# One stage change of a two-layer decoder trunk written out in a fixed order on PE, ACT and DVE

## The chip, the cores and the metric

The kernel runs on one core of one Trainium2 chip. The metric is the device time of one execution in microseconds (us). PE is TensorE (matmul), DVE VectorE, ACT ScalarE, POOL GpSimd, SP the engine that issues the DMAs.

## The reference, cut to what matters

```python
x = sandwich(x, mixer, ...)        # layer 1: mixer = dilated_attention
x = sandwich(x, ffn_second, ...)   # layer 1: swiglu, D_FF = 2816

def sandwich(x, fn, pre_g, post_g, shift, scale, gate, res_w):
    hn = rmsnorm(x, pre_g) * (1 + scale) + shift
    y = rmsnorm(fn(hn), post_g)
    return x + res_w * gate * y

def dilated_attention(h, w_in, w_o, rel_bias):
    ...                                     # three dilations, mixed by their lse
    return o.reshape(B, S, 1024) @ w_o      # 512 tokens, 1024 features

def swiglu(h, w_gate, w_up, w_down):
    return (silu(h @ w_gate) * (h @ w_up)) @ w_down
```

Six such sub-layers run one behind the other (FFN, MLA, FFN, FFN, dilated attention, FFN). All is float32; the kernel splits each operand of a large product into two float32r parts, hi and lo, and sums three products.

## The kernel before

Tokens are the 512 columns, in four tiles of 128 (`TT`); features are 8 tiles of 128 (`KT`). A weight of 128x1024 is loaded by SP (`load`, L124, five `raw` buffers), copied to `whi` by ACT (L134) and subtracted to `wlo` by DVE in two halves (L136); six `whi` and six `wlo` buffers are there. `mm3` (L149 to L151) makes the three products. PSUM has four banks `mm` and four `aux`.

The place of the change is the **transition** behind the dilated stage. The stage's output is `o`, eight pieces (hi and lo each), times `w_o`: for each token tile i and half d of the features, eight times three products of 512 columns. `Mixer.part` makes the first four of the eight (`early`) while attention still runs and DVE copies them to SBUF tiles `y` (L467); `Mixer.tail` makes the rest, and DVE adds (L465). The eighth piece of `o` comes last, from a chain of DMAs and `put_o` (ACT L711, DVE L712). Then, tile by tile: squares on ACT (L316), `y` times the gate (DVE L477), a power on POOL for the root (L324), the residual stream `x` (DVE L505), squares of `x`, and `y` = `x` scaled by its own root (ACT L339 and DVE L340). When two tiles are scaled, PE transposes them (`turn`, L529, 16 transposes), and `modulate` makes `h`, hi and lo, out of each of the eight transposed pieces: DVE L311, ACT L312, DVE L313, or for two of the pieces ACT twice and POOL (L307 to L309).

The next FFN starts with **head units**: unit u is gate and up of 128 hidden features, 48 products over a half of the tokens (256 columns), then silu on ACT (L585), the product (DVE L587), and hi and lo of it (ACT L588, POOL or DVE L590). Three units (`HEAD`) are made in halves, the first half of tokens as soon as tiles 0 and 1 are turned; the others over all 512 columns. Unit 0's weights come in slices (`Sliced`: ACT L67, DVE L71).

Up to the end of `Dil.rest` the order on PE, ACT and DVE is that of the program (`manual_schedule`). In `transition` a scheduler orders these three engines by what it expects to be ready; only SP keeps the program's order.

```python
def transition(self, sub, nxt):        # L479
    ...
    for i in range(TT):
        sub.tail(i)
        self.tile_done(nxt, i)
        if nxt and i % 2:
            self.after(TURN, lambda i=i: self.turn(nxt, i - 1))
    ...
    for lo in (0, HT):
        for u in range(nxt.heads):
            nxt.head(u, lo, lo + HT)
```

Of the kernel before, what the change touches and what calls it, by code (L numbers as in the profile page):

```python
# [14 lines left out]
P = 128  # L15
# [12 lines left out]
UB = 4  # L28
SB = 4
HOT = 400  # L30
HEAD = 3
SPARE = (2, 3)
TURN = 26
START = 4
# [42 lines left out]
class Trunk:  # L77
# [401 lines left out]
    def transition(self, sub, nxt):  # L479
# [15 lines left out]
                    nxt.head(u, lo, lo + HT)  # L495
        self.count(4 * TURN if not nxt or not nxt.late else 0)

    def tile_done(self, nxt, i):

        nc = self.nc  # L500
        r = self.scale_of(self.ss)
        for d in range(2):
            c = slice(d * SEQ, (d + 1) * SEQ)
            x = self.x[i][:, c]
            nc.vector.scalar_tensor_tensor(x, self.y[i][d], r, x, ALU.mult, ALU.add)  # L505
            if not nxt:
                nc.sync.dma_start(self.a["out"][i][:, c], x)
        if nxt:
            self.normal(i, self.y[i])
            if nxt.parks:  # L510
                self.park(i)
# [26 lines left out]
class Ffn:  # L538
# [34 lines left out]
    def gate_up_out(self, ft, lo, hi, banks):  # L573
        t, nc = self.t, self.t.nc
        q = self.group(ft)
        j = ft - GROUPS[q][0]
        if q not in self.g:
            self.g[q] = [[], []]
        if j == len(self.g[q][0]):
            for x in self.g[q]:  # L580
                x.append(t.s(F32R))
        ghi, glo = [x[j][:, lo:hi] for x in self.g[q]]
        n = hi - lo
        s = t.t("silu")[:, :n]
        nc.scalar.activation(s, banks[0], AF.Silu)  # L585
        v = t.t("gg")[:, :n]
        nc.vector.tensor_tensor(v, s, banks[1], ALU.mult)  # L587
        nc.scalar.activation(ghi, v, AF.Copy)  # L588
        eng = nc.gpsimd if n < SEQ and ft < HEAD else nc.vector
        eng.tensor_tensor(glo, v, f(ghi), ALU.subtract)  # L590

    def head(self, ft, lo, hi):
# [38 lines left out]
    def rest(self):  # L631
        t = self.t
        last = len(GROUPS) - 1
        for q, (at, n) in enumerate(GROUPS):
            if q == last - 1:
                t.gates(self)
            for ft in range(max(at, START if t.first is self else HEAD), at + n):
                self.head(ft, 0, SEQ)
                t.pump(3 if t.first is self else 2)
            for i in range(TT if q < last else 0):  # L640
                self.down(q, i)
# [22 lines left out]
class Mixer:  # L664
# [11 lines left out]
    def products(self, b, i, d, js):  # L676
        t = self.t
        for j in js:
            self.out_weights(j)
            t.mm3(  # L680
                b,
                [x[j][:, i * P : (i + 1) * P] for x in self.o],
                [x[:, d * SEQ : (d + 1) * SEQ] for x in self.wo[j]],
                j in (0, self.early),
                j in (self.early - 1, KT - 1),
            )

    def part(self, n):

        i, d = divmod(n, 2)  # L690
        b = self.t.bank()
        self.products(b, i, d, range(self.early))
        self.t.y_part(i, d, b, True, self.busy)

    def tail(self, i):
# [21 lines left out]
class Mla(Mixer):  # L717
# [3 lines left out]
    busy = False  # L721
    early = 3
    waiting = 1
    w_o = "mla_o"

    def head(self, u, lo, hi):
# [242 lines left out]
class Dil(Mixer):  # L969
# [2 lines left out]
    late = False  # L972
    busy = True
    early = 4
    waiting = 1
    w_o = "dil_o"
    BLOCKS = (
        (0, ((0, 384, 128, 0), (1, 256, 256, 0))),
# [457 lines left out]
    def rest(self):  # L1436
        t = self.t
        t.gates(self)
        self.of = []
        self.bias = {}  # L1440
        self.coming, self.raws = self.loads(), []
        self.fetched = self.loaded = self.at = 0
        with t.tc.manual_schedule(engines={PE, ACT, DVE}):
            self.ahead(SLOTS - 2)
            self.biases(0)
            for p in range(7):
                values = [(p, g, j) for g in range(3) for j in range(4) if p in self.BLOCKS_V]
                for n, at in enumerate([(p + 1, u) for u in self.ORDER] + values):
                    self.fetch(self.at + SLOTS + 1 + max(n - 6, 0) % 4)
                    self.slot(p, n)  # L1450
                    self.ahead(self.at + min(SLOTS - 1 + max(n - 6, 0) % 4, SLOTS))
                    self.beside(p, n)
                    if n < 6:
                        self.tile(*at, 0, SEQ)
                    else:
                        self.value_tile(*at)
                    self.behind(p, n)
                    if n < 6 or n % 4 == 1:
                        self.at += 1 if n < 6 else 4
            self.fetch(self.at + SLOTS + 3)  # L1460
            self.slot(7, 0)
            self.ahead(self.at + SLOTS - 1)
            for x in self.of[:4]:
                self.put_o(x)
            self.tile(7, 2, 0, SEQ)
            self.slot(7, 1)
            self.ahead(self.at + SLOTS + 1)
            self.norm_out(self.pairs[6])
            t.new_y()
            self.part(0)  # L1470
            self.later()
            for x in self.of[4:]:
                self.put_o(x)
            self.part(1)
            last = self.pairs[7]
            self.tops(last)
            self.exps(7, (2,))
            self.tops_back(last)
            for i in range(2):
                t.unpark(i)  # L1480
            self.finish(6)
            self.put_o(self.of[-1])
            for n in range(2, 6):
                self.part(n)
            self.exps(7, (3,))
            self.norm_far(last)
            self.exps(7, (0, 1))
            self.norm(last)
            self.turn(7, 2)
            self.part(6)  # L1490
            self.turn(7, 3)
            self.part(7)
            self.turn(7, 0)
            self.weigh(7, 2, 2, 1)
            self.turn(7, 1)
            for n in (3, 0):
                self.weigh(7, n, 2, 1)
            self.norm_out(last)
            self.weigh(7, 1, 2, 1)
            for i in range(2, TT):  # L1500
                t.unpark(i)
            self.finish(7)
            self.put_o(self.of[-1])


def build(tc, a, plan):
    with ExitStack() as ctx:
        t = Trunk(ctx, tc, a)
        subs = [{"ffn": Ffn, "mla": Mla, "dil": Dil}[kind](t, l, i) for kind, l, i in plan]
        first = subs[0]  # L1510
        t.todo = [
            (s.l, 3 * s.i + n, k)
            for s in subs
            for n in ((2,) if s is first else range(3))
            for k in range(KT)
        ]
        with tc.manual_schedule(engines={SP}):
            t.start(first)
        for s, nxt in zip(subs, subs[1:] + [None]):
            with ExitStack() as order:  # L1520
                if s.parks:
                    order.enter_context(tc.manual_schedule(engines={SP}))
                s.rest()
                t.transition(s, nxt)


def bucket(dist):
# [98 lines left out]
```

## Time and profile before

| | |
|---|---|
| median of 3 runs | 2248.38 us (2247.44 to 2249.25) |
| the profiled execution | 2244.7 us, span 2242.9 us |
| PE busy | 2214.4 us, 99% of the span |
| DVE, ACT, POOL busy | 1180.5, 847.5, 109.1 us |
| the transition | about 1842 to 1892 us from the span's start |

The span runs from the first to the last instruction; 1.8 us lie around it. Times in the rows below count from the span's start. Idle time of an engine other than PE costs nothing by itself.

### The profile page before, as it was taken

Reading aid. Unit: us, or ns where it says so; the run is one execution under the profiler, and the core shown is the slowest. Engines: PE = TensorE matmul, PEld = TensorE weight load, DVE = VectorE, ACT = ScalarE, POOL = GpSimd, SP = SyncE. Lnnn points to the kernel's source line nnn. Section 1 sums busy time; section 2 is a strip of 40 time slices with the busy share of each in tenths; the row PEclk is TensorE's granted clock in tenths of the full one; section 3 lists DMA queues with packets and bytes.
Section 4 is the critical chain, followed back from the end, with each engine's and each line's share of the span. In section 5 each row is a group of like instructions: output and inputs, shape, how many; then the busy total and the mean of one; then the engine's idle time right before and its main releaser. Section 6 shows DMA issues by size and latency. Waiting matters only on the chain.

```text
span 2242.9 us, 30146 instructions
## 1 busy us (share of the span) xinstructions
PE 2214.4 (99%) x11354; PEld 1865.8 (83%) x11354; DVE 1180.5 (53%) x2691; ACT 847.5 (38%) x1730; POOL 109.1 (5%) x143
## 2 busy tenths in 40 slices
PE   7999999999999999999999999999999998999998
PEld 5888888977898888898888889888899888888887
DVE  7666565677655356474454464234523467333344
ACT  4432234587633132353222353425342446322232
POOL 0000001210110000020000010000000002000000
PEclk9999999999999999999999999999999999999999
DMA  8575762311255365434654523323342334333231
GB/s 309 158 248 181 200 220 74 109 54 57 69 167 185 106 188 179 131 117 135 181 172 129 160 98 103 112 90 97 85 131 68 104 86 138 92 116 102 76 113 38
DMA packets 124057, 290.34 MB, mean 129 GB/s; under 512 B 44786, under 2 KB 49157, under 8 KB 123910
## 3 DMA queue, kind: packets, MB, share of 16 engines
q1 hardware_dynamic: 123910, 288.41, 41.6%
q8 instruction: 89, 1.46, 0.3%
q14 instruction: 58, 0.48, 0.1%
HBM read 281.76 MB, written 4.49 MB: 128 GB/s over the span
## 4 chain that ended last, share of the span: by engine, by line
PE 92%; ACT 2%; DVE 2%; issue 2%; DMA 1%; POOL 1%; SPq 0%; POOLq 0%; DVEq 0%; ACTq 0%
PE mm L149 28%; PE mm L150 28%; PE mm L151 28%; PE mm L882 1%; PE aux L1298 1%; PE mm L1131 1%; PE aux L1265 1%; PE aux L931 1%; POOL mv L324 1%; PE aux L910 1%; PE aux L529 1%; PE aux L1131 0%; DVE x L505 0%; ACT whi L134 0%; PE aux L150 0%
## 5 line engine op out<-in xcount | busy, mean ns | idle before, releaser
L136 DVE TENSOR_TENSOR wlo<-raw,whi 128x512 fp32r<-128x512 f32 (+1 forms) x714 | 466.6, 690 | 591.5 <-ACT whi L134 587.3
L149 PE MATMUL mm<-s,whi 128*128 128x512 f32 (+1 forms) x1932 | 722.2, 374 | 1.5 <-ACT whi L134 1.5
L150 PE MATMUL mm<-s,whi 128*128 128x512 f32 (+1 forms) x1932 | 718.5, 372 | 0.0
L151 PE MATMUL mm<-s,wlo 128*128 128x512 f32 (+1 forms) x1932 | 718.4, 372 | 0.0
L134 ACT ACTIVATE whi<-raw 128x1024 fp32r<-128x1024 f32 (+1 forms) x357 | 369.3, 1048 | 792.1 <-PE mm L150 545.6
L149 PEld LDWEIGHTS mm<-s,whi 128*128 128x128 f32 x1932 | 364.1, 188 | 69.0 <-issue 3.5
L151 PEld LDWEIGHTS mm<-s,wlo 128*128 128x128 f32 x1932 | 364.2, 189 | 63.7
L150 PEld LDWEIGHTS mm<-s,whi 128*128 128x128 f32 x1932 | 364.3, 189 | 61.5
L149 PE MATMUL mm<-whi,s 128*128 128x512 f32 (+1 forms) x1040 | 406.3, 391 | 0.5 <-ACT s L711 0.5
L150 PE MATMUL mm<-wlo,s 128*128 128x512 f32 (+1 forms) x1040 | 404.4, 389 | 0.0
L151 PE MATMUL mm<-whi,s 128*128 128x512 f32 (+1 forms) x1040 | 404.2, 389 | 0.0
L149 PEld LDWEIGHTS mm<-whi,s 128*128 128x128 f32 x1040 | 210.8, 203 | 36.0 <-issue 1.2
L151 PEld LDWEIGHTS mm<-whi,s 128*128 128x128 f32 x1040 | 210.8, 203 | 34.7 <-DVE s L712 0.2
L150 PEld LDWEIGHTS mm<-wlo,s 128*128 128x128 f32 x1040 | 210.9, 203 | 33.9 <-issue 0.3
L171 DVE CUSTOM_DVE_ANT_0 raw<-raw,cs 128x1024 f32<-128x1024 f32 x130 | 159.4, 1230 | 125.0 <-DMA raw<-w_mod 124.7
L465 DVE TENSOR_TENSOR s<-mm,s 128x512 f32<-128x512 f32 x112 | 76.6, 689 | 118.8 <-PE mm L151 118.6
L324 POOL TENSOR_TENSOR mv<-mv,mhalf 128x1 f32<-128x1 f32 x48 | 36.2, 756 | 1485.9 <-DVE mv L323 1483.4
L1096 ACT ACTIVATE s<-mm 128x128 f32<-128x128 f32 (+3 forms) x109 | 33.2, 359 | 165.0 <-PE mm L151 161.1
L588 ACT ACTIVATE s<-gg 128x512 fp32r<-128x512 f32 (+1 forms) x97 | 57.4, 592 | 40.3 <-DVE gg L587 40.3
L587 DVE TENSOR_TENSOR gg<-silu,mm 128x512 f32<-128x512 f32 (+1 forms) x95 | 59.8, 629 | 9.4 <-ACT silu L585 9.4
L585 ACT ACTIVATE silu<-mm 128x512 f32<-128x512 f32 (+1 forms) x95 | 51.4, 541 | 18.0 <-PE mm L151 18.0
L1212 ACT ACTIVATE u<-u,y 128x128 f32<-128x128 f32 x128 | 49.6, 396 | 22.2 <-DVE y L1190 10.0
(185 smaller groups left out, 1682.8 us busy)
## 6 DMA issues: line engine op xcount, KB each, us to landing
raw<-w_gu SPq DMA_DIRECT2D x168, 512.0 KB, 4.3
raw<-w_mod SPq DMA_DIRECT2D x130, 512.0 KB, 4.5
raw<-w_down SPq DMA_DIRECT2D x88, 512.0 KB, 4.4
raw<-dil_in SPq DMA_DIRECT2D x47, 512.0 KB, 4.2
raw<-dil_v SPq DMA_DIRECT2D x20, 512.0 KB, 4.5
s<-w_mod SPq DMA_DIRECT2D x28, 256.0 KB, 5.8
raw<-w_gu SPq DMA_DIRECT2D x16, 256.0 KB, 3.6
raw<-mla_o SPq DMA_DIRECT2D x8, 512.0 KB, 3.6
```

Of the source, the lines that this page charges most:

```text
L134: self.nc.scalar.activation(hi, raw, AF.Copy)
L136: self.nc.vector.tensor_tensor(lo[:, r], raw[:, r], f(hi[:, r]), ALU.subtract)
L149: mm(out, w[0], m[0], start=first, stop=False)
L150: mm(out, w[0], m[1], start=False, stop=False)
L151: mm(out, w[1], m[0], start=False, stop=last)
L171: nc.vector.tensor_tensor_reduce(raw, raw, self.cs, 1.0, 0.0, ALU.mult, ALU.add, accum_out=t[:, 0:1])
L324: nc.gpsimd.tensor_tensor(v[:, 1:2], v[:, 0:1], self.mhalf[:, 0:1], ALU.pow)
L465: nc.vector.tensor_tensor(y, b, y, ALU.add)
L585: nc.scalar.activation(s, banks[0], AF.Silu)
L587: nc.vector.tensor_tensor(v, s, banks[1], ALU.mult)
L588: nc.scalar.activation(ghi, v, AF.Copy)
L1212: nc.scalar.activation(c, c, AF.Exp, bias=pair["top"][:, g, i, one], scale=-1.0, accum_out=pair["z"][:, g, i, one],)
```

## The change

Behind the dilated stage `transition` is replaced by `line`, which writes the transition out in one order for PE, ACT and DVE and runs under `manual_schedule` of the three. `Mixer.part` takes tiles 1, 2, 3 first and tile 0 last, and leaves tile 0's two sums open in PSUM (`whole`), so that they are squared and gated from there. The last FFN has four head units in halves instead of three. In `line`, `turned` is four transposes into one `aux` bank, `tops` makes u and hi of two pieces of `h` (and for the two pieces of `SPARE` also lo, on POOL), `lows` the lo on DVE; `split` is the ACT copy of a unit's two weights, `split_low` one half of both subtractions on DVE; `head` is a unit's 48 products and returns `out`, the silu and what follows it.

```diff
+MORE = 4
+    def line(self, sub, nxt):
...
+        early, last = range(sub.early, KT - 1), (KT - 1,)
+        b = {(0, d): sub.open[d] for d in range(2)}
...
+        def total(i, d):
...
+            nc.vector.tensor_tensor(y, b[i, d], y, ALU.add)
+            self.square(y, self.t("sq", SB), ss[i][:, d : d + 1])
+        def gate(i, d, src=None):
...
+            nc.vector.tensor_tensor(y, y if src is None else src, gb, ALU.mult)
+        def stream(i, d):
...
+            nc.vector.scalar_tensor_tensor(x, y, r[i], x, ALU.mult, ALU.add)
+            self.square(x, y, sx[i][:, d : d + 1])
+        def scaled(i, n):
...
+            nc.scalar.activation(self.y[i][0], x[0], AF.Copy, scale=n)
+            nc.vector.tensor_scalar(self.y[i][1], x[1], n, None, ALU.mult)
...
+        with self.tc.manual_schedule(engines={PE, ACT, DVE}):
...
+            raw = raws(1)
+            mm(0, early)
+            b[1, 0] = self.bank()
+            sub.products(b[1, 0], 1, 0, early)
+            mm(0, last)
+            sub.products(b[1, 0], 1, 0, last)
+            ss[0] = self.pair()
+            for d in range(2):
+                self.square(b[0, d], self.t("sq", SB), ss[0][:, d : d + 1])
+                gate(0, d, b[0, d])
+            r[0] = self.scale_of(ss[0])
+            total(1, 0)
+            gate(1, 0)
+            b[1, 1] = self.bank()
+            sub.products(b[1, 1], 1, 1, (*early, KT - 1))
+            total(1, 1)
+            stream(0, 0)
+            r[1] = self.scale_of(ss[1])
+            gate(1, 1)
+            stream(0, 1)
+            stream(1, 0)
+            n0 = self.scale_of(sx[0])
+            stream(1, 1)
+            mm(2, (*early, KT - 1))
+            total(2, 0)
+            scaled(0, n0)
+            n1 = self.scale_of(sx[1])
+            w[0].top(0)
+            total(2, 1)
+            w[0].low(0)
+            scaled(1, n1)
+            r[2] = self.scale_of(ss[2])
+            b[3, 0] = self.bank()
+            sub.products(b[3, 0], 3, 0, (*early, KT - 1))
+            a = [turned(0, q) for q in range(KT // 2)]
...
+            b[3, 1] = self.bank()
+            sub.products(b[3, 1], 3, 1, (*early, KT - 1))
...
+            ws = split(1, raw)
+            raw = raws(2)
+            out = head(0)
+            gate(2, 1)
+            split_low(ws, 0)
+            stream(2, 0)
+            split_low(ws, 1)
+            stream(2, 1)
+            out()
+            out = head(1)
+            gate(3, 0)
+            gate(3, 1)
+            n2 = self.scale_of(sx[2])
+            stream(3, 0)
+            ws = split(2, raw)
+            stream(3, 1)
+            scaled(2, n2)
+            split_low(ws, 0)
...
+            split_low(ws, 1)
+            out()
+            out = head(2)
+            scaled(3, n3)
+            if nxt.heads > 3:
+                raw = raws(3)
+                ws = split(3, raw)
...
+            out()
+            if nxt.heads > 3:
+                out = head(3)
+            a = [turned(2, q) for q in range(KT // 2)]
...
+        for u in range(nxt.heads):
+            nxt.head(u, HT, SEQ)
+        self.count(4 * TURN)
...
-        eng = nc.gpsimd if n < SEQ and ft < HEAD else nc.vector
+        eng = nc.gpsimd if n < SEQ and ft < self.heads else nc.vector
...
-        i, d = divmod(n, 2)
+        i, d = divmod((n + 2) % 8 if self.whole else n, 2)
         b = self.t.bank()
         self.products(b, i, d, range(self.early))
+        if self.whole and i == 0:
+            self.open[d] = b
+            return
...
-                t.transition(s, nxt)
+                if s.parks:
+                    nxt.heads = MORE
+                    t.line(s, nxt)
+                else:
+                    t.transition(s, nxt)
```

How the order moves, at three places. In the changed kernel L149 to L151 are L150 to L152, L316 is L317; `split` is L576, `scaled` L535, silu L782 and the hi behind it L785.

PE before, at the first product with the eighth piece of `o` (`s_16142` hi, `s_16143` lo; banks `mm_16163`, `mm_16164` are tile 0, `mm_16221`, `mm_16239` tile 1; 34 products of these four banks stand ahead, from the seventh and earlier pieces):

```order
L151 MATMUL mm_16239<-whi_15857,s_15905 128x512
L149 MATMUL mm_16239<-whi_16171,s_15946 128x512
L149 MATMUL mm_16163<-whi_16188,s_16142 128x512
L150 MATMUL mm_16163<-wlo_16189,s_16142 128x512
L149 MATMUL mm_16164<-whi_16188,s_16142 128x512
L151 MATMUL mm_16163<-whi_16188,s_16143 128x512
L150 MATMUL mm_16164<-wlo_16189,s_16142 128x512
```

PE in the change, at the same point (hi `s_16140`, lo `s_16141`; `mm_16044`, `mm_16061` are tile 0, `mm_16204` the first half of tile 1):

```order
L151 MATMUL mm_16204<-wlo_16188,s_15946 128x512
L152 MATMUL mm_16204<-whi_16187,s_15947 128x512
L150 MATMUL mm_16044<-whi_16214,s_16140 128x512
L151 MATMUL mm_16044<-wlo_16215,s_16140 128x512
L152 MATMUL mm_16044<-whi_16214,s_16141 128x512
L150 MATMUL mm_16061<-whi_16214,s_16140 128x512
L151 MATMUL mm_16061<-wlo_16215,s_16140 128x512
L152 MATMUL mm_16061<-whi_16214,s_16141 128x512
L150 MATMUL mm_16204<-whi_16214,s_16140 128x512
```

Ahead of this point there are now 27 products, not 34: the second half of tile 1 has moved behind it. The three products with hi and lo of one bank now follow each other at once.

PE before, from the last transposes to the first products of the FFN (`s_16147` is `h` hi of piece 0; `s_16270`, `s_16281` unit 0's weights; `whi_16501`, `whi_16508` unit 1's):

```order
L529 MATMUL aux_16387<-ident_81,s_15874 128x128
L529 MATMUL aux_16400<-ident_81,s_15874 128x128
L529 MATMUL aux_16400<-ident_81,s_15872 128x128
L529 MATMUL aux_16400<-ident_81,s_15874 128x128
L149 MATMUL mm_16439<-s_16147,s_16270 128x256
L149 MATMUL mm_16440<-s_16147,s_16281 128x256
L149 MATMUL mm_16497<-s_16147,whi_16501 128x256
L149 MATMUL mm_16498<-s_16147,whi_16508 128x256
L150 MATMUL mm_16439<-s_16155,s_16270 128x256
L151 MATMUL mm_16439<-s_16147,s_16272 128x256
L150 MATMUL mm_16440<-s_16155,s_16281 128x256
```

PE in the change, at unit 0's first products (`s_16145` is `h` hi of piece 0, `s_16153` its lo; `mm_16368` is the second half of tile 3's output):

```order
L150 MATMUL mm_16368<-whi_16214,s_16140 128x512
L151 MATMUL mm_16368<-wlo_16215,s_16140 128x512
L152 MATMUL mm_16368<-whi_16214,s_16141 128x512
L150 MATMUL mm_16426<-s_16145,s_16164 128x256
L151 MATMUL mm_16426<-s_16153,s_16164 128x256
L152 MATMUL mm_16426<-s_16145,s_16166 128x256
L150 MATMUL mm_16427<-s_16145,s_16169 128x256
L151 MATMUL mm_16427<-s_16153,s_16169 128x256
L152 MATMUL mm_16427<-s_16145,s_16171 128x256
L150 MATMUL mm_16426<-s_16146,s_16164 128x256
```

The transposes now stand ahead of twelve products of tile 3, and units 0 and 1 are no longer mixed: each unit's 48 products stand together.

ACT before, around the split of unit 2's two weights (`whi_16625`, `whi_16632`; `x_15942` is the stream of tile 1, `x_16136` of tile 2):

```order
L316 ACTIVATE s_15874,ss_16261<-x_15942 128x512
L67 ACTIVATE s_16281<-raw_16280 128x512
L134 ACTIVATE whi_16625<-raw_16623 128x1024
L339 ACTIVATE s_15873<-x_15942,mv_16264 128x512
L67 ACTIVATE s_16282<-raw_16280 128x512
L134 ACTIVATE whi_16632<-raw_16630 128x1024
L316 ACTIVATE s_15875,ss_16331<-x_16136 128x512
L316 ACTIVATE sq_16354,ss_16353<-s_15877 128x512
```

ACT in the change, around unit 2's two weights (`whi_16552`, `whi_16555`; `silu_16488` is unit 0's, `x_16134` the stream of tile 2, `x_16136` of tile 3):

```order
L317 ACTIVATE s_15875,ss_16479<-x_16134 128x512
L317 ACTIVATE s_15876,ss_16479<-x_16134 128x512
L782 ACT_TABLE_LOAD
L782 ACTIVATE silu_16488<-mm_16426 128x256
L785 ACTIVATE s_16486<-gg_16490 128x256
L317 ACTIVATE s_15877,ss_16549<-x_16136 128x512
L576 ACTIVATE whi_16552<-raw_16422 128x1024
L576 ACTIVATE whi_16555<-raw_16424 128x1024
L317 ACTIVATE s_15878,ss_16549<-x_16136 128x512
L535 ACTIVATE s_15875<-x_16134,mv_16546 128x512
```

Unit 2's weights were split ahead of tile 2's own squares; they now stand behind tile 2's squares, the load of the function table, unit 0's silu and the first square of tile 3's stream.

## Rows read from the trace of the kernel before

**Rows 1.** From the page, its first part: busy time, share of the span and number of instructions of each engine.
```profile
PE 2214.4 (99%) x11354; PEld 1865.8 (83%) x11354; DVE 1180.5 (53%) x2691; ACT 847.5 (38%) x1730; POOL 109.1 (5%) x143
```

**Rows 2.** The timeline of PE in the transition. Columns: start in us, us that the row lasts, engine, line, operation, out<-in, stationary tile, output shape, count; in brackets the idle time ahead of it in us and what ended that. A matmul's row lasts longer than PE needs before the next one can start, so the pace is read from start to start.
```profile
1849.66 0.39 PE L149 MATMUL mm<-whi,s 128*128 128x512 f32 x1
1850.53 0.50 PE L149 MATMUL mm<-whi,s 128*128 128x512 f32 x1 [0.48 <-ACT s L711]
...
1857.97 0.39 PE L149 MATMUL mm<-whi,s 128*128 128x512 f32 x1
1858.20 0.39 PE L150 MATMUL mm<-wlo,s 128*128 128x512 f32 x1
...
1865.04 0.39 PE L151 MATMUL mm<-whi,s 128*128 128x512 f32 x1
1867.07 1.53 PE L529 MATMUL aux<-ident,s 128*128 128x128 f32 x12 [1.64 <-ACT s L339]
1871.30 0.51 PE L149 MATMUL mm<-s 128*128 128x256 f32 x2 [2.70 <-ACT s L312]
...
1871.87 0.28 PE L150 MATMUL mm<-s 128*128 128x256 f32 x1
1871.99 0.28 PE L151 MATMUL mm<-s 128*128 128x256 f32 x1
...
1873.73 0.28 PE L149 MATMUL mm<-s,whi 128*128 128x256 f32 x1
1875.17 0.39 PE L150 MATMUL mm<-s 128*128 128x256 f32 x1 [1.17 <-POOL s L309]
```

**Rows 3.** The table of stretches: busy us and, in brackets, instructions of PE, PE's weight load, DVE, ACT, POOL, then the granted TensorE clock, the DMA share and GB/s.
```profile
1868.00:1872.00 4.00, 1.30 (x12) 1.06 (x11) 3.83 (x10) 3.76 (x12) 0.79 (x2) 1.00 0.44 131
25.00:30.00 5.00, 4.34 (x11) 3.40 (x11) 4.87 (x11) 1.58 (x2) 0.00 (x0) 1.00 0.39 100
```

**Rows 4.** The timeline of ACT in the transition, same columns.
```profile
1858.71 0.61 ACT L67 ACTIVATE s<-raw 128x512 fp32r<-128x512 f32 x1
1859.23 1.05 ACT L134 ACTIVATE whi<-raw 128x1024 fp32r<-128x1024 f32 x1
1860.18 0.71 ACT L339 ACTIVATE s<-x,mv 128x512 f32<-128x512 f32 x1
1860.79 1.05 ACT L134 ACTIVATE whi<-raw 128x1024 fp32r<-128x1024 f32 x1
...
1867.45 1.04 ACT L134 ACTIVATE whi<-raw 128x1024 fp32r<-128x1024 f32 x1
...
1869.01 0.61 ACT L316 ACTIVATE sq<-s 128x512 f32<-128x512 f32 x1
...
1869.62 0.61 ACT L316 ACTIVATE sq<-s 128x512 f32<-128x512 f32 x1
```

**Rows 5.** The timeline of DVE in the transition, same columns.
```profile
1850.51 0.69 DVE L712 TENSOR_TENSOR s<-s 128x512 fp32r<-128x512 f32 x1 [0.76 <-ACT s L711]
...
1859.22 0.22 DVE L323 SCALAR_TENSOR_TENSOR mv<-ss 128x1 f32<-128x1 f32 x2
1859.53 0.69 DVE L465 TENSOR_TENSOR s<-mm,s 128x512 f32<-128x512 f32 x1
1860.14 0.48 DVE L340 TENSOR_SCALAR s<-x,mv 128x512 f32<-128x512 f32 x1
...
1868.19 0.74 DVE L505 SCALAR_TENSOR_TENSOR x<-s,mv,x 128x512 f32<-128x512 f32 x1
1868.85 0.99 DVE L311 TENSOR_SCALAR u<-aux,mA,mS 128x256 f32<-128x256 f32 x2
1869.76 1.28 DVE L477 TENSOR_TENSOR s<-s,gb 128x512 f32<-128x512 f32 x2
...
1877.17 0.42 DVE L313 TENSOR_TENSOR s<-u,s 128x256 fp32r<-128x256 f32 x1
1877.50 0.69 DVE L136 TENSOR_TENSOR wlo<-raw,whi 128x512 fp32r<-128x512 f32 x1
```

**Rows 6.** The timeline of POOL in the transition, same columns.
```profile
1859.46 1.20 POOL L324 TENSOR_TENSOR mv<-mv,mhalf 128x1 f32<-128x1 f32 x2 [4.11 <-DVE mv L323]
...
1873.50 2.31 POOL L309 TENSOR_TENSOR s<-u,s 128x256 fp32r<-128x256 f32 x2 [1.19 <-ACT u L308]
```

**Rows 7.** The timeline of ACT around two loads of its function table: the first behind the first layer's attention projections, the second in this transition.
```profile
448.92 1.28 ACT L888 ACT_TABLE_LOAD   x1
450.22 0.40 ACT L888 ACTIVATE sq<-sq,st 128x128 f32<-128x128 f32 x1
...
1879.64 1.28 ACT L585 ACT_TABLE_LOAD   x1
1882.01 0.38 ACT L585 ACTIVATE silu<-mm 128x256 f32<-128x256 f32 x1 [1.09 <-PE mm L151]
```

**Rows 8.** The timeline of PE at the start of the program, where its first dense products run.
```profile
25.69 1.22 PE L149 MATMUL mm<-s 128*128 128x512 f32 x2 [0.66 <-ACT s L312]
26.70 0.63 PE L150 MATMUL mm<-s 128*128 128x512 f32 x1
27.13 0.63 PE L151 MATMUL mm<-s 128*128 128x512 f32 x1
...
30.11 0.39 PE L151 MATMUL mm<-s,wlo 128*128 128x512 f32 x1
```

More of the change, by code (lines that the diff above doesn't have):

```diff
@@ L636, in rest @@
                 t.gates(self)
-            for ft in range(max(at, START if t.first is self else HEAD), at + n):
+            for ft in range(max(at, START if t.first is self else self.heads), at + n):
                 self.head(ft, 0, SEQ)
@@ L683, in products @@
                 [x[:, d * SEQ : (d + 1) * SEQ] for x in self.wo[j]],
-                j in (0, self.early),
-                j in (self.early - 1, KT - 1),
+                j == 0 or (j == self.early and (i > 0 or not self.whole)),
+                j == KT - 1 or (j == self.early - 1 and (i > 0 or not self.whole)),
             )
     def part(self, n):
-        i, d = divmod(n, 2)
+        i, d = divmod((n + 2) % 8 if self.whole else n, 2)
         b = self.t.bank()
         self.products(b, i, d, range(self.early))
+        if self.whole and i == 0:
+            self.open[d] = b
+            return
         self.t.y_part(i, d, b, True, self.busy)
@@ L723 @@
     waiting = 1
+    whole = False
     w_o = "mla_o"
@@ L974 @@
     early = 4
-    waiting = 1
+    whole = True
     w_o = "dil_o"
@@ L1439, in rest @@
         self.of = []
+        self.open = {}
         self.bias = {}
@@ L1523, in build @@
                 s.rest()
-                t.transition(s, nxt)
+                if s.parks:
+                    nxt.heads = MORE
+                    t.line(s, nxt)
+                else:
+                    t.transition(s, nxt)
 def bucket(dist):
```

96 lines of the change are left out of this document (added).

## The prediction

> **What bounds the kernel now.** I read the page's busy times first: PE is busy 99% of the span [rows 1], so only time in which PE stands still, or work that PE is given, can move the end. The second view is PE's timeline in the transition [rows 2]: the reader is to see where the next product could have started and when it did. A product of 512 columns starts every 0.227 us, one of 256 columns every 0.12 us. Against that pace PE loses 0.64 us at 1850.53 (1850.53 - 1849.66 - 0.23), waiting for the last piece of `o`; 1.80 us at 1867.07 (1867.07 - 1865.04 - 0.23), waiting for ACT's scaling of tile 1; some 2.87 us at 1871.30, waiting for the first piece of `h` (twelve transposes at 0.113 us end at 1868.43); and 1.32 us at 1875.17, waiting for POOL's lo of the third piece. That is **6.63 us**, and nothing beyond it is to be had. The table of stretches shows the same: PE busy 1.30 of 4 us from 1868 to 1872, while DVE and ACT are busy 3.83 and 3.76 [rows 3]. So the two engines that make `h` bound this stage. Third, the timelines of ACT, DVE and POOL [rows 4 to 6] give what one instruction takes from start to start: on DVE 0.61 us for any operation of two 512-column inputs, 0.66 for the stream update, 0.455 for a top of 256 columns, 0.33 for a lo of 256; on ACT 0.61 for a square with its readout and for a scaling, 0.52 for half a slice, 0.95 for a whole weight; on POOL 0.6 for a power, about 1.15 for a lo.
>
> **The change, part by part.** I lay the new order along these steps, starting at 1850.53, when the hi of the last `o` is ready; that chain of DMAs is not touched.
>
> *Cover ahead of the last `o`.* 27 products stand there instead of 34, so PE gets there 7 x 0.227 = 1.59 us earlier and waits 0.64 + 1.59 = **2.23 us**. Bounds: 1.9 if the chain gains from DVE's two fewer copies, 2.5 if it loses as much.
>
> *Hi and lo of one bank at once.* The lo is ready at 1851.20 [rows 5]; the third product would start at 1850.53 + 2 x 0.227 = 1850.98, so **0.28 us** with the signal. Before, a product of the other bank filled this.
>
> *Tile 0 whole in PSUM.* Two copies and two adds of 0.61 us leave DVE. DVE waits for the squares at that point, so this is worth nothing on the path; without that cover it would be at most 2.4 us of DVE, part of the bounds below. PE's 96 products stay 96.
>
> *Scaling of tile 1.* PE from 1850.53: 9 products and 0.28, to 1852.86; tile 1's second half, 12, to 1855.59; tile 2, 24, to 1861.04; tile 3's first half, 12, to 1863.77. The other side: from 1855.6 on the add (behind a gate, 1856.8), the square 0.8 (1857.6), the sum and POOL's 0.6 (1858.5), two streams of tile 1 and the sum between them (1860.8), its square (1861.5), and then on ACT in a row a square 0.62, the scaling of tile 0 0.61, half a slice 0.52, a square 0.62, the scaling of tile 1 0.72: 1864.6. PE waits **0.88 us** (1.80 before). Bounds 0 and 1.8.
>
> *First pieces of `h`.* 16 transposes of 0.113 and 12 products of tile 3 take PE to 1869.2, when the first pieces are long made; unit 0 starts then instead of at 1871.30. The sixth product of its fifth piece needs the last slice of unit 0's weights, which DVE has behind 6 tops (2.73), 4 lows (1.32), five 512-column operations (3.1) and a wait of 0.4 for ACT, from its first top at 1865.3 to 1873.0 with the tail; PE comes at 1869.2 + 29 x 0.12 = 1872.7: about **0.35 us**. Bounds 0 and 1.3 (POOL's wait as before).
>
> *Unit 2's weights.* Here I see a new wait. Unit 0 ends at 1869.2 + 5.76 + 0.35 = 1875.3, unit 1 at **1881.1**. Unit 2's split stands on ACT behind tile 3's first stream, which DVE has behind unit 0's silu. DVE, from its first top at 1865.3, has 6 tops (2.73), 6 lows (2.0), ten 512-column operations (6.05), two streams (1.32), a sum (0.08) and a wait of 0.4 before tile 2's stream is done: 1877.98. Then ACT's square (1878.67), its table load with what follows it 1.30 [rows 7] (1879.97), silu 0.38 (1880.35), DVE's product, two gates, a sum and the stream (1882.8), ACT's square (1883.5), the split 1.05 (1884.55). PE starts unit 2 at 1884.6: **3.5 us** lost. Before, unit 2 was split by 1868.5 [rows 4] and nobody waited. The sixth product needs the second weight's lo: 0.95 more on ACT and 0.69 on DVE, so about **1.1 us** more. Bounds of the two together 3.0 and 5.6, from 5% on the steps and the rivals' ends. Unit 3's weights come 0.3 us ahead of PE.
>
> *Second halves.* The last 16 transposes now stand directly ahead of unit 0's second half; before, first-half products of other units stood between them. What is left of the wait for the first pieces is bounded by 0 and 2.87, the wait at the same step before; I take **0.9**, near the lower end, since tops and lows are all that DVE has to do there, and POOL's 1.15 ends its wait.
>
> *A fourth unit in halves.* 48 products of 0.227 become 96 of 0.12: **0.61 us** of PE, with no bounds to speak of. POOL gets two more lows of about 1.15 and DVE one subtraction of 0.61 less: nobody waits for these before the down products. SP issues unit 3's two loads ahead of the gate row's load and the later ones; they need buffers that DVE frees at 1872 to 1877, some 4 us before they are needed, so nothing.
>
> *Sum.* 2.23 + 0.28 + 0.88 + 0.35 + 3.5 + 1.1 + 0.9 = 9.24 us of waits, against 6.63; with 0.61 of work **3.2 us more**. The profiled execution took 2244.7 us, so 2247.9 for the same; the runs' median lies 3.7 above it at 2248.38, and on that scale I say **2251.6 us**. The lowest bounds give 1.9 + 0.28 + 0 + 0 + 3.0 + 0 + 0.61 - 6.63 = -0.8, the highest 2.5 + 0.28 + 1.8 + 1.3 + 5.6 + 2.87 + 0.61 - 6.63 = +8.3.
>
> **The rivals.** A measurement of this kernel can tell about 0.2%, 4.5 us.
>
> *No change that can be told* is my forecast, +1 to +4.4 us. For it: every wait saved is paid again, one at the start and one at unit 2.
>
> [...]
>
> *Slower, since the table load costs more than its row.* In this transition silu starts 1.09 us after the load's end, put down to PE [rows 7]; were that the load's, the chain to unit 2 would be 1.09 longer: +4.3, and with a little of the other bounds past 4.5. Against it: behind the first load the next instruction starts 0.02 us after its end. [...]
>
> *Slower by the chain alone*: DVE and ACT each lose some steps in the fixed order, and unit 3's 0.3 us of reserve is gone too. With 1.5 us on the way to unit 2 that is +4.7 and more.
>
> *Faster.* The order does all that it can: the waits of 0.88, 0.35, 3.5, 1.1 and 0.9 vanish. Then 2.23 + 0.28 + 0.61 - 6.63 = -3.5 us, 2244.9. For a gain of over 4.5 us the wait for `o` would have to shrink as well.
>
> **How the numbers follow.** The clock 0.12, the table load 0.05, the longer chain 0.14: slower by over 0.2% 0.31. My forecast 0.52 and the better half of the bounds (-4.4 to +1) 0.12: within 0.2% 0.64. Beyond the faster rival 0.05. The range leaves out about 2 in 10: from 2247.5 (-0.9, the lowest bounds) to 2256.0 (+7.6, the clock and a longer chain together).
>
> **What would show it.** Right: PE waits about 2.2 us for the last `o`, under 1 us ahead of the transposes, under 0.5 us in unit 0, which starts some 2 us earlier, and 3 to 4 us ahead of unit 2's first product, put down to ACT's split; ACT's row of that split stands behind a square of tile 3. Wrong: no wait at unit 2, or a pace of 0.24 us for 256 columns behind it (the clock), or a gap behind the table load. If the time falls by more than 4 us, the chain over unit 0's silu was not the last to arrive.

## The result, and the profile after

The change takes 2253.41 us (median of 11 runs, 2251.37 to 2254.41); the kernel before, timed beside it, 2247.44 (11 runs, 2246.27 to 2249.25). The ratio is 1.0026, 95% interval 1.0017 to 1.0035: **slower by 6.0 us**, which a measurement of this kernel can tell. The profiled execution of the change took 2252.88 us, span 2251.1. The page's first part, which answers to [rows 1]:

```profile
PE 2218.1 (99%) x11402; PEld 1870.7 (83%) x11402; DVE 1180.2 (52%) x2687; ACT 849.0 (38%) x1732; POOL 108.5 (5%) x145
```

PE has 48 more products and 3.7 us more busy time; the busy times of DVE, ACT and POOL are within 1.5 us of before. The loss shows on PE's timeline (columns as in [rows 2], which these rows answer):

```profile
1848.12 0.39 PE L152 MATMUL mm<-whi,s 128*128 128x512 f32 x1
1852.38 0.80 PE L150 MATMUL mm<-whi,s 128*128 128x512 f32 x1 [3.87 <-ACT s L911]
1852.97 0.63 PE L151 MATMUL mm<-wlo,s 128*128 128x512 f32 x1
...
1858.72 0.39 PE L150 MATMUL mm<-whi,s 128*128 128x512 f32 x1
...
1868.25 0.27 PE L542 MATMUL aux<-ident,s 128*128 128x128 f32 x1
1868.70 1.86 PE L542 MATMUL aux<-ident,s 128*128 128x128 f32 x15 [0.17 <-ACT s L535]
...
1876.50 0.28 PE L151 MATMUL mm<-s 128*128 128x256 f32 x1
1876.87 0.39 PE L152 MATMUL mm<-s 128*128 128x256 f32 x1
1877.09 0.28 PE L150 MATMUL mm<-s 128*128 128x256 f32 x1
...
1884.88 0.28 PE L152 MATMUL mm<-s,wlo 128*128 128x256 f32 x1
1889.01 0.48 PE L150 MATMUL mm<-s,whi 128*128 128x256 f32 x1 [3.86 <-ACT whi L576]
...
1891.71 0.41 PE L150 MATMUL mm<-s,whi 128*128 128x256 f32 x1
...
1892.56 0.29 PE L151 MATMUL mm<-s,whi 128*128 128x256 f32 x1
```

Two waits of 4 us are to be seen, at the last `o` (1852.38) and at unit 2 (1889.01), and behind each of them products that take nearly twice the time of those in [rows 2]: 0.43 us for 512 columns from 1852.97 on, 0.23 again from 1858.72; 0.21 for 256 behind 1889.01, 0.12 again from 1892.56. The table of stretches (columns as in [rows 3]) has the granted clock below 1.00 at these two places:

```profile
1850.00:1855.00 5.00, 2.62 (x6) 2.10 (x7) 1.53 (x3) 1.32 (x3) 0.00 (x0) 0.66 0.86 309
1855.00:1860.00 5.00, 5.00 (x16) 3.92 (x16) 2.59 (x5) 1.41 (x4) 0.55 (x1) 0.66 1.03 412
...
1890.00:1895.00 5.00, 5.00 (x32) 4.77 (x33) 3.34 (x7) 4.12 (x8) 1.60 (x2) 0.74 0.50 170
```

The prediction's terms beside this execution, each from start to start less 0.227, 0.12 or 0.113 us for every product or transpose between:

| what PE loses, us | predicted | measured |
|---|---|---|
| wait for the last `o` | 2.23 | 4.03 |
| hi and lo of one bank; measured: 15 slow products, 1852.38 to 1858.72 | 0.28 | 2.94 |
| scaling of tile 1 | 0.88 | 0.34 |
| unit 0's fifth piece | 0.35 | 0.35 |
| unit 2's first product | 3.5 | 4.01 |
| lo of unit 2's weights; measured: with 13 slow products, to 1892.56 | 1.1 | 1.99 |
| second halves, 1902.53 to 1910.94 | 0.9 | 0.84 |
| sum | 9.24 | 14.50 |

14.50 + 0.61 - 6.63 is 8.5; the spans differ by 8.2. So the account closes, but on 8.2, not on the 6.0 of the runs: the two profiled executions are not equally typical, which the first experiment shows.

The chain to unit 2's split, on ACT and, in the second fence, DVE and POOL:

```profile
1882.66 1.28 ACT L782 ACT_TABLE_LOAD   x1
1883.96 0.39 ACT L782 ACTIVATE silu<-mm 128x256 f32<-128x256 f32 x1
...
1887.29 0.63 ACT L317 ACTIVATE s<-x 128x512 f32<-128x512 f32 x1 [2.05 <-DVE x L530]
...
1887.92 1.99 ACT L576 ACTIVATE whi<-raw 128x1024 fp32r<-128x1024 f32 x2
```

```profile
1885.91 0.68 DVE L324 SCALAR_TENSOR_TENSOR mv<-ss 128x1 f32<-128x1 f32 x1
...
1885.32 1.26 POOL L787 TENSOR_TENSOR s<-gg,s 128x256 fp32r<-128x256 f32 x1 [5.56 <-ACT s L785]
```

It runs as predicted: table load, silu, tile 3's stream on DVE, its square, split. Only DVE's one-column sum (L324) takes 0.68 us there; the median of its 48 rows in this execution is 0.16.

### The profile page after: what moved, and what is told of

Its sections match the earlier page's. It is cut to its first block, busy times and chain, and to the rows that moved or that the text cites. A ratio compares the mean times of both kernels' runs of the same rounds, so it can differ in the third digit from the quotient of the medians.

```text
span 2251.1 us, 30245 instructions
## 1 busy us (share of the span) xinstructions
PE 2218.1 (99%) x11402; PEld 1870.7 (83%) x11402; DVE 1180.2 (52%) x2687; ACT 849.0 (38%) x1732; POOL 108.5 (5%) x145
## 3 DMA queue, kind: packets, MB, share of 16 engines
q8 instruction: 89, 1.46, 0.3%
## 5 line engine op out<-in xcount | busy, mean ns | idle before, releaser
L137 DVE TENSOR_TENSOR wlo<-raw,whi 128x512 fp32r<-128x512 f32 (+1 forms) x702 | 459.7, 693 | 582.4 <-ACT whi L135 578.2
L150 PE MATMUL mm<-s,whi 128*128 128x512 f32 (+1 forms) x1948 | 725.3, 373 | 6.2 <-ACT whi L576 3.9
L152 PE MATMUL mm<-s,wlo 128*128 128x512 f32 (+1 forms) x1948 | 721.8, 371 | 0.0
L151 PE MATMUL mm<-s,whi 128*128 128x512 f32 (+1 forms) x1948 | 721.6, 370 | 0.0
L135 ACT ACTIVATE whi<-raw 128x1024 fp32r<-128x1024 f32 (+1 forms) x351 | 363.1, 1048 | 781.5 <-PE mm L151 526.5
L150 PEld LDWEIGHTS mm<-s,whi 128*128 128x128 f32 x1948 | 367.6, 189 | 72.9 <-ACT whi L576 4.1
L152 PEld LDWEIGHTS mm<-s,wlo 128*128 128x128 f32 x1948 | 367.7, 189 | 63.4 <-DVE wlo L584 0.6
L151 PEld LDWEIGHTS mm<-s,whi 128*128 128x128 f32 x1948 | 368.0, 189 | 61.0
L150 PE MATMUL mm<-whi,s 128*128 128x512 f32 (+1 forms) x1040 | 407.5, 392 | 3.9 <-ACT s L911 3.9
L151 PE MATMUL mm<-wlo,s 128*128 128x512 f32 (+1 forms) x1040 | 405.5, 390 | 0.0
L152 PE MATMUL mm<-whi,s 128*128 128x512 f32 (+1 forms) x1040 | 405.1, 390 | 0.0
L150 PEld LDWEIGHTS mm<-whi,s 128*128 128x128 f32 x1040 | 211.5, 203 | 39.5 <-ACT s L911 4.3
L152 PEld LDWEIGHTS mm<-whi,s 128*128 128x128 f32 x1040 | 211.5, 203 | 34.8 <-DVE s L912 0.2
L151 PEld LDWEIGHTS mm<-wlo,s 128*128 128x128 f32 x1040 | 211.6, 203 | 34.2 <-issue 0.3
L466 DVE TENSOR_TENSOR s<-mm,s 128x512 f32<-128x512 f32 x104 | 71.4, 690 | 118.9 <-PE mm L152 118.8
L785 ACT ACTIVATE s<-gg 128x512 fp32r<-128x512 f32 (+1 forms) x98 | 57.6, 588 | 49.0 <-DVE gg L784 49.0
L782 ACT ACTIVATE silu<-mm 128x512 f32<-128x512 f32 (+1 forms) x96 | 51.6, 537 | 13.0 <-PE mm L152 12.9
```

The source lines that it names most:

```text
L135: self.nc.scalar.activation(hi, raw, AF.Copy)
L137: self.nc.vector.tensor_tensor(lo[:, r], raw[:, r], f(hi[:, r]), ALU.subtract)
L150: mm(out, w[0], m[0], start=first, stop=False)
L151: mm(out, w[0], m[1], start=False, stop=False)
L152: mm(out, w[1], m[0], start=False, stop=last)
L466: nc.vector.tensor_tensor(y, b, y, ALU.add)
```

## The experiments

Times are medians; of before those of the runs beside it: 2247.97 (27 runs) for the first four, 2248.32 (33) for the next four, 2248.38 (21) for the last two. Before's own median thus moves by up to 0.9 us from one set of runs to the next. The differences to the change below are taken from its 2253.41, timed beside a before of 2247.44, and are good to about 1 us.

**The kernel before, once more.** No edit.

> The kernel before, profiled a second time, to see what its own chain to the last `o` does from one execution to the next. In the profile of before, the last add ahead of `o` starts at 1849.06 us; in that of the change at 1850.97, with every product before it at the same place. Theory A (the chain of small transfers varies by itself): here it starts later than in the first profile, by up to 2 us, and the wait for `o` is 0.5 to 2.5 us. Rival B (the change makes the transfers late): it starts at 1849.1 again, within 0.3. In both the span goes up by what `o` is late, and no product behind the wait runs at the 0.43 us pace as long as the wait stays under 3 us.

Measured: 2248.73 us, span 2246.9. DVE's last add ahead of `o`, in the first profile of before, in this one and in the change's:

```profile
1849.06 0.69 DVE L1318 TENSOR_TENSOR s<-aux,s 128x512 f32<-128x512 f32 x1 [6.00 <-DMA s<-d]
```

```profile
1851.29 0.69 DVE L1318 TENSOR_TENSOR s<-aux,s 128x512 f32<-128x512 f32 x1 [5.63 <-DMA s<-d]
```

```profile
1850.97 0.69 DVE L1519 TENSOR_TENSOR s<-aux,s 128x512 f32<-128x512 f32 x1 [5.62 <-DMA s<-d]
```

Theory A: 2.23 us later, with a wait of 2.57, both just past what was expected. In the nine other profiles below this add starts between 1850.54 and 1851.93: the first profile of before, from which I predicted, is the one that stands out, and its 2244.7 us is below every timed run (lowest of 27: 2246.17). So `o` comes late in the kernel before too, and the change is not needed for it. The last line of the expectation failed, though. PE in this execution, and a stretch of it:

```profile
1852.76 0.79 PE L149 MATMUL mm<-whi,s 128*128 128x512 f32 x1 [2.41 <-ACT s L711]
1853.35 0.63 PE L150 MATMUL mm<-wlo,s 128*128 128x512 f32 x1
...
1874.91 0.51 PE L149 MATMUL mm<-s 128*128 128x256 f32 x2 [2.69 <-ACT s L312]
...
1876.64 0.41 PE L151 MATMUL mm<-s 128*128 128x256 f32 x1
```

```profile
1875.00:1880.00 5.00, 4.75 (x26) 4.45 (x27) 4.91 (x12) 4.76 (x12) 3.52 (x5) 0.66 0.48 143
```

The clock falls in the kernel before as well, behind a wait of 2.57 us for `o` (granted 0.74 from 1850 to 1855) and again behind the wait of 2.87 us for the first piece of `h` (0.66 from 1875 to 1880), the same wait at which the first profile kept its pace of 0.12 us [rows 2]. In the same account before loses 10.8 us here (2.57 for `o`, 1.55 of slow products, 1.80, 2.87, and 2.00 up to 1879.79). Against this execution the change is 14.50 + 0.61 - 10.8 = 4.3 us slower, and the spans say 4.2. The runs' 6.0 lies between 4.2 and 8.2.

**The splits of units 2 and 3 earlier.**

```diff
             split_low(ws, 1)
+            ws = split(2, raw)
+            raw = raws(3)
             stream(2, 1)
+            split_low(ws, 0)
+            split_low(ws, 1)
             out()
...
             stream(3, 0)
-            ws = split(2, raw)
+            ws = split(3, raw)
             stream(3, 1)
...
-            if nxt.heads > 3:
-                raw = raws(3)
-                ws = split(3, raw)
```

> The change, with the split of unit 2's weights moved ahead of tile 2's second stream and that of unit 3's ahead of tile 3's second stream. Theory A (the wait of 4.0 us ahead of unit 2 and the slow 13 products behind it, 2.0 us, come from the place of the split): both go; unit 2 then waits some 0.5 us for the bank that unit 0's silu frees, since silu stands 2 us of splitting later, and unit 3 about 1.7 us for its own weights: 6.0 - 0.5 - 1.7 = 3.8 us less, 2249.6. Rival B (DVE's and ACT's work as a whole bounds the stage, and the wait moves on): the same time within 1 us, with 4 us of PE's idle time found at unit 3 or ahead of the second halves.

Measured: 2248.81 us (2247.96 to 2249.58), 4.6 less than the change; against before 1.0005 (0.9996 to 1.0014). The longest of PE's waits in the transition (engine and line waiting, releaser: us in total, times, longest):

```profile
PE mm L150 <- ACT s L910: 3.8, 1, 3.8
PE mm L150 <- ACT silu L781: 1.0, 1, 1.0
PE mm L150 <- DVE gg L783: 0.6, 1, 0.6
```

Theory A, with 0.8 us more gained than expected: unit 2 starts without a wait. The 1.6 us that remain stand at unit 3 and belong to the banks that unit 1's silu and product free, not to its weights, as I had it; the size was the same.

**Nine products of cover back at `o`.**

```diff
-            b[1, 0] = self.bank()
-            sub.products(b[1, 0], 1, 0, early)
+            mm(1, early)
             mm(0, last)
...
-            b[1, 1] = self.bank()
-            sub.products(b[1, 1], 1, 1, (*early, KT - 1))
+            sub.products(b[1, 1], 1, 1, last)
```

> The change, with the nine early products of tile 1's second half put back ahead of the wait for the last `o`: 36 products of cover. Theory A (the clock falls after a stillness of some 4 us, and the chain over ACT and DVE from `o` to the scaling of tile 1 bounds the stretch): the wait for `o` falls by 2.0 us, products behind it run at 0.227 us, the stretch from `o` to the last 15 transposes falls from 16.3 to about 14.2 us, and the wait ahead of the transposes grows to 2 to 3 us; the time falls by the 2.1 us of the chain alone, 2251.3. Rival B (the cover itself is what was lost): 2.0 of wait and 2.7 of clock are both gained, 2248.7. Rival C (the clock falls there whatever the wait): pace 0.43 us behind it, the same time as the change.

Measured: 2251.38 us (2251.04 to 2252.03), 2.0 less. PE:

```profile
1852.64 0.50 PE L150 MATMUL mm<-whi,s 128*128 128x512 f32 x1 [1.67 <-ACT s L909]
...
1864.86 0.33 PE L542 MATMUL aux<-ident,s 128*128 128x128 f32 x1 [0.75 <-ACT s L535]
1866.61 1.85 PE L542 MATMUL aux<-ident,s 128*128 128x128 f32 x15 [1.42 <-ACT s L535]
```

Theory A: products behind `o` keep their pace (granted clock 1.00 from 1850 to 1860), and from `o` to the 15 transposes it is 13.97 us instead of 16.32. What the wait for `o` gave back, PE loses ahead of the transposes (0.91 + 1.64, by starts). So 2.35 us is what the slow products had cost on the chain: 1852.64 to 1866.61 here, 1852.38 to 1868.70 in the change. Unit 2's wait (4.01) and slow products stay (granted 0.61 and 0.70 from 1885 to 1895), and there are 25 of these in this profile for the change's 13.

**Both waits filled.** 18 and 34 products whose sums nobody reads:

```diff
+            idle = self.bank("aux")
+            for n in range(18):
+                nc.tensor.matmul(idle, sub.o[0][0][:, :P], sub.wo[6][0][:, :SEQ], start=True, stop=True)
             mm(0, last)
...
             out = head(1)
+            idle = self.bank("aux")
+            for n in range(34):
+                nc.tensor.matmul(idle[:, :HT], nxt.w[1][0][0][:, n % 8, :], self.h[0][n % 8][:, :HT], start=True, stop=True)
```

> The change, with 18 products of 512 columns put into the wait for `o` and 34 of 256 columns into the wait ahead of unit 2; nobody reads their sums. The waits stay as long, only PE has work in them. Theory A (the clock falls because PE stands still there): every product behind runs at 0.227 and 0.12 us; the chain from `o` is 2.1 us shorter, the slow products at unit 2 give back 1.2 less what the two weights' lo then wait for again; 2 to 3 us less in all, 2250.4 to 2251.4. Rival B (standing still is not the cause): paces of 0.43 and 0.21 us stay behind both places, and the time is that of the change or up to 1 us more.

Measured: 2250.17 us (2249.25 to 2250.91), 3.2 less, with 52 products more. PE:

```profile
1848.25 4.24 PE L603 MATMUL aux<-whi,s 128*128 128x512 f32 x18
1852.33 0.39 PE L150 MATMUL mm<-whi,s 128*128 128x512 f32 x1
...
1865.27 0.27 PE L542 MATMUL aux<-ident,s 128*128 128x128 f32 x1
1865.90 1.86 PE L542 MATMUL aux<-ident,s 128*128 128x128 f32 x15 [0.36 <-ACT s L535]
...
1882.20 4.24 PE L666 MATMUL aux<-s,whi 128*128 128x256 f32 x34
1886.28 0.35 PE L150 MATMUL mm<-s,whi 128*128 128x256 f32 x1
```

Theory A, with 0.2 us more gained than expected: standing still is the cause, since work without any use takes the slow products away at both places (granted clock 1.00 in every stretch of 5 us from 1850 to 1910). Counted from the end of ACT's row that makes the hi of the last `o`, 1851.90 here and 1852.33 in the change, it is 14.00 us to the 15 transposes instead of 16.37: the clock's part is 2.37 by this count, 2.35 by the last experiment. Unit 2's first 13 products lose 1.13 us here (1886.28 to 1888.97), the prediction's 1.1 for the lo, so the clock's part of the 1.99 was 0.86. With the 2.35 at `o` that is 3.2 us, the difference of the medians; the two profiles differ by 3.6, and `o` comes 0.43 us earlier in this one.

**The table load earlier.**

```diff
             ws = split(1, raw)
+            nc.scalar.activation(self.t("sq", SB)[:, :4], self.mhalf[:, 0:4], AF.Silu)
             raw = raws(2)
```

> The change, with a silu of four columns put behind unit 1's split, where ACT waits 1.5 us for DVE: the load of the function table, 1.28 us, moves there. Theory A (the load lies on the path to unit 2's split): silu of unit 0 starts 1.3 us earlier, at about 1882.7 on the scale of the change's profile, the wait ahead of unit 2 falls from 4.0 to 2.7 us, and the time by 1.3, to 2252.1; if the clock then stays at its higher level behind the shorter wait, by about 1 more, 2251.2. Rival B (the load is hidden, since ACT waits there for DVE or PE in any case): the wait stays 4.0 us and the time is that of the change.

Measured: 2251.85 us (2251.22 to 2252.64), 1.6 less. ACT:

```profile
1879.17 1.28 ACT L652 ACT_TABLE_LOAD   x1
1880.46 0.21 ACT L652 ACTIVATE sq<-mhalf 128x4 f32<-128x4 f32 x1
...
1883.14 0.36 ACT L783 ACTIVATE silu<-mm 128x256 f32<-128x256 f32 x1
```

PE:

```profile
1888.19 0.38 PE L150 MATMUL mm<-s,whi 128*128 128x256 f32 x1 [2.45 <-ACT whi L576]
```

Theory A's first half: the load lay on the path, and PE's wait ahead of unit 2 fell from 4.01 to 2.60 (by starts). The clock fell behind it all the same (granted 0.73 from 1890 to 1895).

**Cover and early splits together.** Both edits above.

> The two edits in one: nine more products of cover ahead of the last `o`, and the splits of units 2 and 3 moved ahead. They took 2.0 and 4.6 us from the change. Theory A (two separate losses, one at `o` by the clock and one at unit 2 by the split): both add, 2253.4 - 6.6 = 2246.8, some 1 us under the kernel before. Rival B (they are one loss: what is won at `o` is waited for again at unit 2 or 3): 2248 to 2249, no better than the earlier split alone.

Measured: 2247.76 us (2246.68 to 2249.76), against before 0.9998 (0.9989 to 1.0007): between the two expectations, 1.0 above A's and 0.2 below B's range, so this time alone doesn't separate them. The profile shows why A's sum is not reached: unit 3 still waits 1.11 and 0.77 us for its banks, and the granted clock behind these is 0.69 from 1890 to 1895. With the early splits alone it held at 1.00 there, behind waits of 1.14 and 0.77.

**Reordered.** Both edits, and these; further adds, slices and their lo move along with them (at the marks):

```diff
             r[0] = self.scale_of(ss[0])
             total(1, 0)
-            gate(1, 0)
...
             total(1, 1)
             stream(0, 0)
+            stream(0, 1)
+            w[0].top(0)
+            w[1].top(0)
             r[1] = self.scale_of(ss[1])
+            gate(1, 0)
             gate(1, 1)
-            stream(0, 1)
-            stream(1, 0)
             n0 = self.scale_of(sx[0])
+            stream(1, 0)
             stream(1, 1)
...
             out = head(1)
+            ws = split(3, raw)
             gate(3, 0)
```

> Both edits, and the steps of tiles 0 and 1 in another order: the adds of both halves of tile 1 ahead of its gates, both streams of tile 0 ahead of those gates, unit 0's first half slices on ACT in its idle time, unit 3's split directly behind unit 0's silu. With both edits PE waits 0.9 and 1.6 us ahead of the transposes, where the chain of DVE and ACT from `o` ends last. Theory A (that chain's order sets its length, since DVE waits 1 us for ACT's square ahead of tile 1's gates and ACT 1 us for the streams): it gets some 2 us shorter, and the 1.7 us at unit 3 go: 2246.8 - 2.3 = 2244.5. Rival B (the time that both engines need in all sets it): 2246 to 2247.

Measured: 2246.44 us (2245.28 to 2247.74), 1.3 less than the last: inside B's range, 1.9 above A's 2244.5. Its row of the transposes:

```profile
1864.37 1.86 PE L542 MATMUL aux<-ident,s 128*128 128x128 f32 x15 [0.59 <-ACT s L535]
```

From `o` (1852.22) it is 12.15 us to the transposes, 1.8 less than with cover alone, so the order did set the chain's length, by 1.8 of the 2 us that A expected. Part of it is paid again in units 0 and 1, where PE waits 0.73, 0.38 and 0.38 us for DVE's lo.

**Reordered, with the early table load.**

> The reordered kernel, with the silu of four columns behind unit 1's split as well. Theory A: unit 2's first product waits about 0.4 us for the bank that unit 0's silu and product free; the load of the table 1.3 us earlier takes that wait away, 0.4 us less than without it, 2244.1, which the time alone can't tell but the row of the wait can. Rival B: the wait ends by something else (the split of unit 2's weights) and stays.

Measured: 2245.31 us (2244.98 to 2246.78), **0.9987 of before (0.9978 to 0.9996)**: 3.0 us faster than before and 8.1 than the change. The wait at unit 2 (0.36 in the reordered kernel) is gone, as in A. In this profile the clock fell behind a wait of 1.78 us for `o` (granted 0.87 and 0.79 from 1850 to 1860), where behind 1.91 us in the last one it hadn't (1.00).

**Three units in halves.** The change with `MORE = 3`.

> The change with three head units in halves, as before the change: the fourth unit's two halves, 96 products of 256 columns at 0.12 us, become 48 of 512 at 0.227. Theory A (a unit in halves costs its pace and nothing else): 0.6 us less, 2252.8, with the waits at `o`, unit 2 and in the second halves as they are, each within 0.3 us. Rival B (unit 3 is the cover for tile 3's scaling): the last 16 transposes, 5.8 us earlier, wait for ACT's scaling of tile 3, by 1 to 3 us: 2253.5 to 2255.5.

Measured: 2252.28 us (2251.42 to 2253.68); 1.0018 of before (1.0009 to 1.0027). 1.1 less than the change where 0.6 was expected; the intervals overlap, so the time only says that rival B's cost isn't there. In its profile the waits at `o` (4.14) and unit 2 (4.02) are as in the change, but 28 slow products (0.21 us for 256 columns) follow the second.

**Reordered, table early, 7 products in the wait for `o`.**

> The reordered kernel with the early load of the table, and 7 products of 512 columns, whose sums nobody reads, in the wait for the last `o`, which took 1.8 us there. In its profile the products from 1853.7 to 1856.7 us ran at the slow pace behind that wait, in the one without the early table load they did not, behind a wait of 1.9. Theory A (the clock falls behind some of the executions' waits at `o`): no product behind runs at 0.43 us in the profile, and the time falls by 0.3 to 1 us, 2244.3 to 2245.0. Rival B (the chain over DVE and ACT hides what the slow products cost): the time is the same within 0.3 us, 2245.3.

Measured: 2245.02 us (2244.55 to 2246.58), 0.9985 of before (0.9976 to 0.9994). No product behind `o` runs at 0.43 us, but 0.3 us is what both sides allowed: inconclusive.

## Why the prediction was right, and where it was wrong

**Right: the mechanism.** The prediction took away the waits for the first piece of `h` and for POOL, and put one ahead of unit 2 in their place, through silu and tile 3's stream. That wait is there, put down to ACT's split, and moving the split takes it away. Unit 0's 0.35, the second halves' 0.84 and the 1.13 for the lo without the slow clock are the predicted sizes. One sign did not come: unit 0 should have started some 2 us earlier. From the end of ACT's row for the hi of `o` it is 20.8 us to unit 0 in the change (1873.15) and 20.8 in the first profile of before (1871.30); with the pace kept it is 18.45 (filled). And the time lies in the range through its upper part, which was there for the clock and a longer chain; the forecast's own sum, 2251.6, is 1.8 us low, and the difference to before is 6.0 for 3.2.

**The wait for `o`, 4.03 for 2.23.** The term itself holds: against the second profile of before, where `o` comes 0.4 us later than in the change's, the wait is 1.46 us longer, for 1.59 expected. The other 1.8 us are `o` coming late, and the second profile shows that in the kernel before as well. I read them off one execution that was faster than any timed one. Its distance of 3.7 us to the median stood in my own text, and I carried it as an offset without asking what makes it; the second profile answers with a longer wait for `o` and a slower clock behind it.

**Wrong: the clock.** This is the step that failed, and why the change is slower by more than 0.2% and not "no change that can be told". I gave it 0.12, at one place, unit 2, and 2.1 us. That price is an estimate from the program's start, where PE runs 4.42 us at 0.43 us for 512 columns [rows 8]: 4.42 x (1 - 0.227/0.43). The granted clock reads 1.00 there [rows 3], so it is not shown that this pace was the clock's. The clock falls at two places, and the one at `o`, to which I gave nothing, costs 2.35 us. At unit 2 it costs 0.86 in the change's profile, since slower products wait less for the lo and only 13 are slow. How many are slow differs: with 25 (cover) and 28 (three units), behind the same wait, the whole loss is 3.09 and 3.37 us and the clock's part 1.96 and 2.24, about the estimate. The clock's part of the range's +7.6 rests on the 2.1, which no run shows as such; the runs showed 2.35 us at `o` and 0.86 to 2.24 at unit 2 in its place, and a pace of 0.21 us for 256 columns where I had named 0.24. My argument against it was one row, a wait of 2.87 us behind which the pace held at 0.12 us [rows 2]. The same wait of the same kernel was followed by slow products in the second execution. With the pace kept at both places (filled) the kernel is 2.2 us slower than before, inside the forecast's +1 to +4.4. That idle time ahead of the products does it is shown by the filled kernel, with 3.2 us less.

**Mis-sized: unit 2, 4.01 for 3.5.** DVE's one-column sum at 1885.91 ends at 1886.59; POOL's lo of unit 0, begun at 1885.32, ends at 1886.58. In the profiles of eight of its variants DVE's sum takes 0.68 to 0.70 us at this place too, and ends within 0.02 us of POOL's lo. I counted 0.08 for it; the next row starts 0.61 behind it, so 0.5 us more on the chain, for 0.5 more of wait. That POOL holds DVE is my estimate from these rows; no run takes POOL's step away, and why it would is not shown.

**Scaling of tile 1, 0.34 for 0.88.** Too large by 0.4: with the pace kept, the same order gives 0.52 (filled, 1865.27 to 1865.90). In the change the slow products hold up PE and the chain over ACT and DVE alike, so the wait there is no larger. Cover's 2.55 is that much larger because nine products, 2.04 us, no longer stand between `o` and the transposes.

**The table load.** The rival that it costs more than its row is refuted: silu follows 0.02 us behind its end, and moving it took 1.41 us off the wait.

The sum for the runs: 3.2 predicted, 0.5 for DVE's sum and 3.2 for the clock, less what the clock costs the kernel before, which its second profile shows at 1.4 us on the way from `o` to the transposes (17.92 for 16.54) and 0.7 behind the first piece of `h` (2.00 for 1.32): 4.8, for 6.0 measured. The 1.2 between them is not explained; each size comes from one execution. The granted clock as a mean over a whole run shows the difference as well. It is 0.995 to 0.997 in all 11 runs of the change. In 81 runs of the kernel before it is 0.999 in 10 (median 2246.7 us), as in the first profile, 0.998 in 51 (2248.3) and 0.995 to 0.997 in 20 (2249.1): most of them lose some time to it, and fewer lose as much.

## What to carry to other kernels

Profile the kernel before twice, and ask what makes the gap between its profiled execution and its median before it is carried as an offset. Where PE stands still, price the products behind the wait at the lower clock too (here 0.43 us for 512 columns instead of 0.23, and 0.21 for 256 instead of 0.12), and look at whether the chain over the other engines gets longer by it. Where an order is written by hand, fill the bounding chain from the late input first: adds and streams ahead of gates, splits and table loads in idle time, together with more products ahead of the late input, turned a loss of 6.0 us into a gain of 3.0.

## What the runs showed that I had not expected

- The granted clock fell, to 0.61 to 0.93 in a stretch of 5 us, behind waits of very different length: 3.9 us and more (seven waits in five profiles, none of which it held behind; those of three units by the pace, 0.43 and 0.21 us), 2.57 and 2.87 (before, second profile), 2.60 (table early), 1.78 (reordered with the table), and 1.11 with 0.77 (cover and early splits). It held at 1.00 behind 2.87 (before, first profile), 1.82 (cover), 1.94 (cover and early splits), 1.91 (reordered), and 1.14 with 0.77 (early splits). Behind some the slow products begin late: with the early splits PE starts at 1852.39 and slows at 1853.45.
- The chain of small transfers to `o` took some 2 us longer in one execution of the same kernel than in another; from issue to use, `x<-z` took 1.7 us in the first profile of before (issued at 1840.26, used at 1841.96) and 2.6 in the second (1841.97, 1844.57). That is 0.9 us of the difference; steps ahead of `x<-z` make up the rest, since it is issued 1.7 us later already.
- POOL's lo of 128x256 took 1.26 us beside DVE's 512-column products (1885.32 in the change) and 0.74 where DVE was idle (1892.77, 1898.00).
